# Rotating an 8192 x 8192 matrix: three output buffers, part of the grid in PSUM, and the first output of a macro tile gathered row tile by row tile

## The chip, the cores and the metric

The kernel runs on one core of one Trainium2 chip. The metric is device time in microseconds (us). TensorE is called PE here, VectorE DVE, ScalarE ACT, and SyncE SP. A DMA of this kernel always moves 2 MB (128 partitions of 16 KB). DMAs started by SP run on queue q1, those started by ACT on q10; both queues are served by the same 16 DMA engines.

## The reference

The matrix is rotated by 90 degrees, counterclockwise; no arithmetic is done on its elements.

```python
x = np.random.randn(8192, 8192).astype(np.float32)
k = 1
out = np.rot90(x, k)          # out[i, j] = x[j, 8191 - i]
```

Every element is read once and written once: 268 MB each way.

## The kernel before

The matrix is cut into 16 macro tiles of R = 1024 rows by W = 4096 columns. A macro tile is loaded as T = 8 row tiles of 128 rows (load m = 8 kk + t for row tile t of macro tile kk), and stored as J = 8 outputs (output n = 8 kk + j), each of 512 columns of the macro tile, which are 512 rows of the result. There are 128 loads and 128 outputs, 2 MB each.

Every engine has its own list of instructions, written out by hand, and waits on semaphores:

- **SP** issues the loads in order (L119). A load goes into one of the `bufs`: the first eight turn through four buffers, later ones through buffers 0 and 1. It waits until the load that used the buffer before has been copied out (`s_copy`).
- **DVE** has two kinds of work. `place(m)` (L125 to L131) waits for load m and copies it, 4096 elements per partition in one instruction (L128), into `grid`, a square of 8 by 8 chunks of 512 elements. Macro tiles are written along rows and along columns of the square in turn, so that load n + 8 takes exactly the chunks that output n has just left. Staging (L143) copies from a column of the grid 128 columns of all eight row tiles, in reversed order, into one of two `stage` tiles of 1024 elements: four such copies per output. DVE's order is: place the first eight loads; then for each output four stage copies, then `place(n + 8)`.
- **PE** turns the 128 x 128 blocks of a stage tile by eight transposes (L163, each a matmul with the identity) into PSUM. `ps` holds four quarter outputs, all of PSUM. PE needs a free half of `ps` (`s_free`) for every two stage tiles, and each filled stage (`s_full`).
- **ACT** waits until its output buffer is free (`s_store`, or at the end `s_copy`), copies two quarter outputs at a time, 2048 elements, from PSUM to the buffer (L189, two copies per output), and issues the store (L195). Outputs turn through buffers 2 and 3; the last eight also use 0 and 1.

So DVE can run ahead of ACT by the four quarters in PSUM and two in the stages, and stores can be two deep.

Of the kernel before, what the change touches and what calls it, by code (L numbers as in the profile page):

```python
# [6 lines left out]
P = 128  # L7


R = 1024  # L10
T = R // P
W = 4096
G = 4
J = W // (G * P)


CH = G * P
F = G * R

LOOP = 8  # L20
PAIR = 2


def whole_reads(nc):
# [17 lines left out]
def kernel(tc: tile.TileContext, x: bass.AP, k: bass.AP, out: bass.AP):  # L42
    nc = tc.nc
    assert k == 1, f"only k=1 supported, got {k}"
    nc.at_finalize(whole_reads)

    N, M = x.shape
    dt = x.dtype
    macros = [(r0, c0) for r0 in range(0, N, R) for c0 in range(0, M, W)]
    n_out = len(macros) * J  # L50
    n_load = len(macros) * T

    with tc.tile_critical():  # L53
        ident = nc.alloc_sbuf_tensor("ident", [P, P], dt)
        bufs = [nc.alloc_sbuf_tensor(f"buf{i}", [P, F], dt) for i in range(4)]
        grid = nc.alloc_sbuf_tensor("grid", [P, T * J * CH], dt)
        stage = [nc.alloc_sbuf_tensor(f"stage{i}", [P, R], dt) for i in range(2)]
        ps = nc.alloc_psum_tensor("ps", [P, 4 * R], mybir.dt.float32)

        s_id = nc.alloc_semaphore("s_id")  # L60
        s_land = [nc.alloc_semaphore(f"s_land{i}") for i in range(4)]
        s_store = [nc.alloc_semaphore(f"s_store{i}") for i in range(4)]
        s_copy = nc.alloc_semaphore("s_copy")
        s_full = nc.alloc_semaphore("s_full")
        s_pe = nc.alloc_semaphore("s_pe")
        s_act = nc.alloc_semaphore("s_act")
        s_free = nc.alloc_semaphore("s_free")

        def load_buf(m):
            return m % 4 if m < T else m % 2

        def out_buf(n):
            return 2 + n % 2 if n < n_out - J else (2 + n) % 4

        def slots(t, kk):

            g = grid[:].rearrange("p (a b c) -> p a b c", a=T, b=J)
            return g[:, t, :, :] if kk % 2 == 0 else g[:, :, t, :]  # L80

        def column(j, kk):

            g = grid[:].rearrange("p (a b c) -> p a b c", a=T, b=J)
            return g[:, :, j, :] if kk % 2 == 0 else g[:, j, :, :]

        landed = [0] * 4
        land_wait = []
        for m in range(n_load):
            landed[load_buf(m)] += 16  # L90
            land_wait.append(landed[load_buf(m)])

        with nc.Block() as block:

            @block.gpsimd
            def _(e):
                e.memset(ident[:], 0.0).then_inc(s_id, 1)  # L97
                e.wait_ge(s_id, 1)
                e.affine_select(  # L99
                    out=ident[:],  # L100
                    in_=ident[:],
                    compare_op=mybir.AluOpType.not_equal,
                    fill=1.0,
                    base=0,
                    pattern=[[-1, P]],
                    channel_multiplier=1,
                ).then_inc(s_id, 1)

            @block.sync
            def _(e):  # L110
                last = {}
                for m in range(n_load):
                    b = load_buf(m)
                    if b in last:
                        e.wait_ge(s_copy, last[b] + 1)
                    last[b] = m
                    r0, c0 = macros[m // T]
                    r0 += m % T * P
                    e.dma_start(  # L119
                        out=bufs[b][:], in_=x[r0 : r0 + P, c0 : c0 + W]  # L120
                    ).then_inc(s_land[b], 16)

            @block.vector
            def _(e):
                def place(m):  # L125
                    b = load_buf(m)
                    e.wait_ge(s_land[b], land_wait[m])
                    e.tensor_copy(  # L128
                        out=slots(m % T, m // T),
                        in_=bufs[b][:].rearrange("p (j c) -> p j c", c=CH),  # L130
                    ).then_inc(s_copy, 1)  # L131

                for t in range(T):
                    place(t)
                for n in range(n_out):
                    kk, j = divmod(n, J)
                    for w in range(G):
                        g = n * G + w
                        if w == 0:
                            e.wait_ge(s_copy, T * (kk + 1))  # L140
                        if g >= 2:
                            e.wait_ge(s_pe, g - 1)
                        e.tensor_copy(  # L143
                            out=stage[g % 2][:].rearrange("p (t c) -> p t c", c=P),
                            in_=column(j, kk)[:, :, w * P : (w + 1) * P][:, :, ::-1],
                        ).then_inc(s_full, 1)
                    if n + T < n_load:
                        e.drain()
                        place(n + T)

            @block.tensor
            def _(e):
                turns = e.alloc_register("turns")
                e.wait_ge(s_id, 2)
                e.reg_mov(turns, n_out * G // LOOP)
                with e.While(lambda: e.snap(turns) > 0):
                    for b in range(LOOP):
                        if b % PAIR == 0:
                            e.wait_ge(s_free, 1).then_inc(s_free, -1)
                        e.wait_ge(s_full, 1).then_inc(s_full, -1)  # L160
                        at = (b // PAIR % 2 * PAIR + PAIR - 1 - b % PAIR) * R
                        for t in range(T):
                            i = e.transpose(  # L163
                                ps[:, at + t * P : at + (t + 1) * P],
                                stage[b % 2][:, t * P : (t + 1) * P],
                                ident[:],
                            )
                        i.then_inc(s_pe, 1)
                    e.reg_sub(turns, turns, 1)

            @block.scalar
            def _(e):
                stored = [0] * 4
                e.sem_inc(s_free, 2)
                for n in range(n_out):
                    kk, j = divmod(n, J)
                    b = out_buf(n)
                    if stored[b]:
                        e.wait_ge(s_store[b], stored[b])
                    else:  # L180
                        e.wait_ge(
                            s_copy, 1 + max(m for m in range(n_load) if load_buf(m) == b)
                        )
                    for h in range(0, G, PAIR):
                        p = (n * G + h) // PAIR
                        e.wait_ge(s_pe, n * G + h + PAIR)  # L186
                        at = p % 2 * PAIR * R
                        to = (G - PAIR - h) * R
                        e.copy(  # L189
                            bufs[b][:, to : to + PAIR * R], ps[:, at : at + PAIR * R]  # L190
                        ).then_inc(s_act, 1)
                        e.wait_ge(s_act, p + 1).then_inc(s_free, 1)  # L192
                    r0, c0 = macros[kk]
                    top = M - c0 - (j + 1) * G * P
                    e.dma_start(  # L195
                        out=out[top : top + G * P, r0 : r0 + R].rearrange(
                            "(g m) f -> m g f", g=G
                        ),
                        in_=bufs[b][:].rearrange("m (g f) -> m g f", g=G),
                    ).then_inc(s_store[b], 16)  # L200
                    stored[b] += 16
                for b in range(4):
                    e.wait_ge(s_store[b], stored[b])


# [33 lines left out]
```

## Time and profile before

| | before |
|---|---|
| median of 3 runs | 1273.86 us (1273.26 to 1273.86) |
| the profiled execution: its own time | 1274.23 us |
| its span | 1272.4 us |
| mean granted PE clock | 0.762 |
| PE busy | 722.3 us (57%), 4096 matmuls |
| DVE busy | 627.9 us (49%), 640 copies |
| ACT busy | 479.2 us (38%), 256 copies |
| DMA | 537.00 MB, 422 GB/s over the span |
| a load, issue to landing | 14.5 us (median of 128) |
| a store, issue to landing | 15.7 us (median of 128) |

The span reaches from the first to the last instruction that the profiler saw; the time of the execution is somewhat longer. Times in the timeline are microseconds from the start of the span. A timeline line gives start, duration, engine (a q behind its name means the engine's sequencer, here issuing a DMA), source line, operation, output and input with their shapes, how many instructions are merged, and in brackets the idle time before and what ended it. A line of the waits gives who waited, for whom, us in total, number of times, the longest. In the windows each engine's busy time stands with the number of its instructions in brackets; the last three columns are the granted PE clock, the share of the DMA engines that was busy, and GB/s moved.

### The profile page before, as it was taken

The page shows a single profiled execution, that of the slowest core. Times are in us where ns is not written, and L with a number is a line of the kernel's source. Part 1 is how long each engine was busy: PE and PEld are TensorE (multiplying, and loading weights), DVE is VectorE, ACT ScalarE, POOL GpSimd, SP SyncE. Part 2 cuts the span into 40 slices and gives each one's busy share as a digit, 9 for nine tenths or more (in the row PEclk, how much of TensorE's full clock was granted, in tenths as well). Part 3 has the DMA queues.
Part 4 walks back from the last instruction along what each step waited for, and adds up shares of the span by engine and source line. Part 5 has one row for each costly group of instructions (what it writes and reads, how often), then busy time and mean ns, then how long its engine had stood idle before and what let it go on. Part 6 is the DMA issues. An engine that isn't in the chain of part 4 may idle for free.

```text
span 1272.4 us, 11079 instructions
## 1 busy us (share of the span) xinstructions
PE 722.3 (57%) x4096; PEld 686.5 (54%) x4096; DVE 627.9 (49%) x640; ACT 479.2 (38%) x257; POOL 0.7 (0%) x6
## 2 busy tenths in 40 slices
PE   0446566565665665556655655655655556556664
PEld 0445556555654555545655655545655555546664
DVE  3644545544455445544554445544555445544453
ACT  0233443344333433343333433344333433344365
POOL 0000000000000000000000000000000000000000
PEclk9986767768677677786777687786687786786798
DMA  9999999999999999999999999999999999999989
GB/s 396 379 430 429 430 429 429 430 430 428 429 431 429 430 429 430 429 430 430 426 426 425 414 424 423 425 421 416 429 426 417 430 430 429 429 429 422 419 361 387
DMA packets 36878, 537.00 MB, mean 422 GB/s; under 512 B 4096, under 2 KB 4096, under 8 KB 4096
## 3 DMA queue, kind: packets, MB, share of 16 engines
q1 hardware_dynamic: 18432, 268.44, 50.1%
q10 hardware_dynamic: 18432, 268.44, 49.7%
q14 instruction: 14, 0.11, 0.0%
HBM read 268.44 MB, written 268.44 MB: 422 GB/s over the span
## 4 chain that ended last, share of the span: by engine, by line
DMA 74%; ACT 20%; issue 1%; ACTq 1%; PE 0%
DMA out_dram<-buf 74%; ACT buf L189 20%; ACTq L195 0%; PE ps L163 0%; ACTq L192 0%; ACT L189 0%; ACTq L186 0%
## 5 line engine op out<-in xcount | busy, mean ns | idle before, releaser
L163 PE MATMUL ps<-ident,stage 128*128 128x128 f32 x4096 | 722.3, 357 | 537.1 <-PEq L160 536.6
L163 PEld LDWEIGHTS ps<-ident,stage 128*128 128x128 f32 x4096 | 686.5, 192 | 572.7 <-issue 571.9
L189 ACT COPY buf<-ps 128x2048 f32<-128x2048 f32 x256 | 477.9, 1867 | 733.2 <-DMA out_dram<-buf 712.5
L143 DVE COPY stage<-grid 128x1024 f32<-128x1024 f32 x512 | 343.1, 690 | 592.3 <-PE ps L163 591.0
L128 DVE COPY grid<-buf 128x4096 f32<-128x4096 f32 x128 | 293.6, 2294 | 38.0 <-DMA buf<-in_x_dram 26.8
L189 ACT ACT_TABLE_LOAD x1 | 1.3, 1283 | 49.4 <-PE ps L163 49.4
L99 POOL TENSOR_SCALAR_AFFINE_SELECT ident<-ident 128x128 f32<-128x128 f32 x1 | 0.3, 294 | 0.2 <-POOL ident L97 0.2
L97 POOL MEMSET ident<- 128x128 f32 x1 | 0.2, 205 | 0.5 <-SPq L53 0.5
L220 POOL MEMSET const-bfloat16-1.0<- 128x1 bf16 x1 | 0.1, 103 | 0.0
L220 POOL MEMSET const-uint8-127<- 128x1 uint8 x1 | 0.1, 102 | 0.0
L220 POOL MEMSET const-float32-0.0<- 128x1 f32 x1 | 0.1, 99 | 0.2 <-issue 0.2
L220 POOL MEMSET const-float32-1.0<- 128x1 f32 x1 | 0.1, 99 | 0.0
## 6 DMA issues: line engine op xcount, KB each, us to landing
buf<-in_x_dram SPq DMA_DIRECT2D x128, 2048.0 KB, 14.5
out_dram<-buf ACTq DMA_DIRECT2D x128, 2048.0 KB, 15.7
```

Source lines behind the costliest of these rows:

```text
L97: e.memset(ident[:], 0.0).then_inc(s_id, 1)
L99: e.affine_select(out=ident[:], in_=ident[:], compare_op=mybir.AluOpType.not_equal, fill=1.0, base=0, pattern=[[-1, P]], channel_multiplier=1,
L128: e.tensor_copy(out=slots(m % T, m // T), in_=bufs[b][:].rearrange("p (j c) -> p j c", c=CH),).then_inc(s_copy, 1)
L143: e.tensor_copy(out=stage[g % 2][:].rearrange("p (t c) -> p t c", c=P), in_=column(j, kk)[:, :, w * P : (w + 1) * P][:, :, ::-1],).then_in ...
L163: i = e.transpose(ps[:, at + t * P : at + (t + 1) * P], stage[b % 2][:, t * P : (t + 1) * P], ident[:],)
L189: e.copy(bufs[b][:, to : to + PAIR * R], ps[:, at : at + PAIR * R]).then_inc(s_act, 1)
L220: nc = _bacc.Bacc("TRN2", target_bir_lowering=False, num_devices=1)
```

## The change

- **Buffers.** There are five `bufs` in place of four. The first nine loads (0 to 8) turn through buffers 0, 1, 2; later ones through 0 and 1. Outputs turn through 2, 3, 4; the last eight use all five.
- **Grid.** Room for the fifth buffer comes from the grid: its corner of 2 by 2 chunks (row and column 6 and 7 of the square) lies in PSUM (`corner`, half of PSUM). Two of the four chunks of SBUF so freed remain at the end of `grid` and serve as the two stages. `ps` shrinks to the other half of PSUM, two quarter outputs.
- **Half stages.** A stage now holds 512 elements, half of a quarter output. An output takes eight stage copies, each with four transposes. PE still waits for a free part of `ps` once for eight transposes.
- **Corner copies.** A stage copy or a place that reaches into the corner becomes two instructions, one for the SBUF part and one for the PSUM part. This concerns rows 6 and 7 of a macro tile (3072 and 1024 elements), and the odd halves of outputs j = 6 and 7 (256 and 256).
- **First output.** Output j = 0 of a macro tile is staged by row tile: a half stage takes the 512 elements of one row tile. For macro tile 0 every row tile is staged straight from its load buffer as it lands, and placed after that. For later macro tiles row tiles 0 to 6 come from the grid and the last from its load buffer; this stands in DVE's order behind the last output of the macro tile before, ahead of the place of that last row tile. ACT copies such an output with a regrouped write.
- **ACT** copies one quarter output at a time (1024 elements), four copies per output.

```diff
-        bufs = [nc.alloc_sbuf_tensor(f"buf{i}", [P, F], dt) for i in range(4)]
-        grid = nc.alloc_sbuf_tensor("grid", [P, T * J * CH], dt)
-        stage = [nc.alloc_sbuf_tensor(f"stage{i}", [P, R], dt) for i in range(2)]
-        ps = nc.alloc_psum_tensor("ps", [P, 4 * R], mybir.dt.float32)
+        bufs = [nc.alloc_sbuf_tensor(f"buf{i}", [P, F], dt) for i in range(5)]
+        grid = nc.alloc_sbuf_tensor("grid", [P, (T * J - 2) * CH], dt)
+        corner = nc.alloc_psum_tensor("corner", [P, 4 * CH], mybir.dt.float32)
+        ps = nc.alloc_psum_tensor("ps", [P, 2 * R], mybir.dt.float32)
...
         def load_buf(m):
-            return m % 4 if m < T else m % 2
+            return m % 3 if m <= T else (m + 1) % 2
 
         def out_buf(n):
-            return 2 + n % 2 if n < n_out - J else (2 + n) % 4
+            e = n - (n_out - J)
+            if e < 0:
+                return 2 + (n + 1) % 3
+            free = [load_buf(n_load - 2), load_buf(n_load - 1)]
+            free += [out_buf(n_out - J - 3 + i) for i in range(3)]
+            return free[e % 5]
...
+                    e.drain()
                     e.wait_ge(s_land[b], land_wait[m])
+                    for at, n, v in pieces(*((0, t) if kk % 2 else (t, 0)), J, kk % 2):
+                        i = e.tensor_copy(out=v, in_=a[:, at : at + n, :])
+                    i.then_inc(s_copy, 1)
+
+                def to_stage(srcs):
+
+                    nonlocal half
+                    if half >= 2:
+                        e.wait_ge(s_pe, half - 1)
+                    for at, v in srcs:
+                        s = stage(half)[:, at * P : at * P + v.shape[1] * v.shape[2]]
+                        i = e.tensor_copy(
+                            out=s.rearrange("p (n c) -> p n c", n=v.shape[1]),
+                            in_=v[:, :, ::-1],
+                        )
+                    i.then_inc(s_full, 1)
+                    half += 1
+
+                def first(kk):
+
+                    for t in range(T):
+                        m = kk * T + t
+                        b = load_buf(m)
+                        if kk == 0 or t == T - 1:
+                            e.wait_ge(s_land[b], land_wait[m])
+                            v = bufs[b][:, :CH].rearrange("p (n c) -> p n c", n=1)
+                        else:
+                            e.wait_ge(s_copy, m + 1)
+                            v = chunks(*((0, t) if kk % 2 else (t, 0)), 1, False)
+                        to_stage([(0, v)])
+                        if kk == 0 or t == T - 1:
+                            place(m)
+
+                first(0)
                 for n in range(n_out):
                     kk, j = divmod(n, J)
...
+                    if j:
+                        e.wait_ge(s_copy, T * (kk + 1))
+                        for w in range(G):
+                            for t in range(0, T, H):
+                                to_stage(
...
+                    if kk + 1 < len(macros):
+                        if j < J - 1:
+                            place(n + T)
+                        else:
+                            first(kk + 1)
...
-                    for h in range(0, G, PAIR):
-                        p = (n * G + h) // PAIR
-                        e.wait_ge(s_pe, n * G + h + PAIR)
-                        at = p % 2 * PAIR * R
-                        to = (G - PAIR - h) * R
-                        e.copy(
-                            bufs[b][:, to : to + PAIR * R], ps[:, at : at + PAIR * R]
-                        ).then_inc(s_act, 1)
-                        e.wait_ge(s_act, p + 1).then_inc(s_free, 1)
+                    for h in range(G):
+                        g = n * G + h
+                        e.wait_ge(s_pe, 2 * g + 2)
+                        src = ps[:, g % 2 * R : (g % 2 + 1) * R]
+                        if j == 0:
+                            src = src.rearrange("p (t g c) -> p t g c", t=2, g=G)
+                            dst = bufs[b][:].rearrange(
+                                "p (g t c) -> p t g c", g=G, t=T
+                            )[:, 2 * h : 2 * h + 2]
+                        else:
+                            dst = bufs[b][:, (G - 1 - h) * R : (G - h) * R]
+                        e.copy(dst, src).then_inc(s_act, 1)
+                        e.wait_ge(s_act, g + 1).then_inc(s_free, 1)
```

`pieces` and `chunks` give the access patterns of a row or column of the grid, cut where it passes into the corner.

## The prediction

> **What bounds the kernel now.** I read first the page's slices and queues, then the waits, then the start in 2 us windows, then the chain and the end by its single instructions.
>
> ```profile
> span 1272.4 us, 11079 instructions
> GB/s 396 379 430 429 430 429 429 430 430 428 429 431 429 430 429 430 429 430 430 426 426 425 414 424 423 425 421 416 429 426 417 430 430 429 429 429 422 419 361 387
> q1 hardware_dynamic: 18432, 268.44, 50.1%
> q10 hardware_dynamic: 18432, 268.44, 49.7%
> ```
>
> Loads (q1) and stores (q10) together fill the DMA engines. The plateau of 429 to 430 GB/s is their limit; no engine's work shows there. 537 MB at 430 is 1249 us, so at most some 23 us can be won: at the start (396, 379), in the dips of the middle (full engines, slower packets; the change has no hold on them), and at the end (361, 387).
>
> ```profile
> 50.00:52.00 2.00, 1.98 (x13) 1.74 (x11) 1.90 (x2) 1.99 (x2) 0.00 (x0) 1.00 0.62 262
> 52.00:54.00 2.00, 0.86 (x8) 0.89 (x9) 1.60 (x3) 1.88 (x2) 0.00 (x0) 1.00 0.60 123
> 54.00:56.00 2.00, 2.00 (x19) 1.77 (x18) 1.49 (x3) 1.14 (x2) 0.00 (x0) 1.00 0.73 303
> 58.00:60.00 2.00, 1.06 (x10) 1.09 (x11) 1.40 (x3) 1.22 (x1) 0.00 (x0) 1.00 0.90 254
> ```
>
> The last column is GB/s: loads have run out of buffers and no store is there yet. From 46 to 62 us the windows miss 811 x 2 us / 429 = **3.8 us** of transfer.
>
> ```profile
> 593.93 15.70 DMA out_dram<-buf
> 613.60 15.75 DMA out_dram<-buf
> ```
>
> This chain follows every second store: 19.7 us for two stores and two loads, **4.92 us per 2 MB transfer**, 9.85 per load and store.
>
> ```profile
> ACT buf L189 <- DMA out_dram<-buf: 712.5, 120, 10.3
> DVE grid L128 <- DMA buf<-in_x_dram: 26.8, 9, 8.2
> ```
>
> ACT waits for old stores at 120 outputs, DVE for loads only 9 times: loads are ahead, stores behind. How far, at the end:
>
> ```profile
> 1192.07 0.33 SPq L119 DMA_DIRECT2D buf<-in_x_dram  x1
> buf<-in_x_dram SPq DMA_DIRECT2D x1, 2048.0 KB, 14.4
> 1202.75 3.85 ACT L189 COPY buf<-ps 128x2048 f32<-128x2048 f32 x2 [5.97 <-DMA out_dram<-buf]
> 1212.64 3.85 ACT L189 COPY buf<-ps 128x2048 f32<-128x2048 f32 x2 [6.04 <-DMA out_dram<-buf]
> ```
>
> Load 126, the last but one, lands at 1192.1 + 14.4 = 1206.5. Counted back from the last issue, 116 stores have landed at 1202.7 and 117 at 1212.6: at 1206.5 it is 116.4. The **lead of loads over stores is 127 - 116.4 = 10.6**, and 243.4 transfers are done. The last store is issued at 1261.9 and takes 9.0: landed 1270.9, **64.4 us after load 126**.
>
> **The change, part by part.**
>
> *Start.* Store 0 no longer waits for place(7) and four stage copies. Load 7 lands at 42.4 (place(7) starts at 42.46); then one 128x512 stage copy. DVE's two sizes, 2.29 us for 4096 and 0.69 for 1024, give 0.52 ns an element and 0.155 fixed: 0.42. Four cold transposes: 16 take about 3.6 before, so 0.95. One ACT copy of 1024. ACT has one size, 1.87 for 2048; half is 0.93, all fixed 1.87; with DVE's fixed part it is 1.01, which I take. Store 0 is issued near 45 instead of 54.6; the table load of 1.28 comes earlier, hidden behind loading. Loads 8, 9 and 10 are under way, 15 us of cover. Gap closed: **-3.8**.
>
> *Middle.* DVE gives 512 stage copies of 0.69 for twice as many of 0.42, ACT 256 of 1.87 for 512 of 1.01. Per output: DVE 8 x 0.42 + 2.3 = 5.7, ACT 4 x 1.01 + 0.4 + issue 0.8 = 5.2, under the period of 9.85: nothing, while it holds. Corner copies touch PSUM, for which DVE has no row: the near bound is SBUF's 0.69 for 1024, the other ACT's PSUM pace 0.91 ns, 1.09; I take 1.09. ACT's regrouped write for a first output has no row either; equal cost, hidden in mid-run. The place of a macro tile's last row moves behind eight more stage copies; queued behind it are the next tile's place, its load on SP, and output 1's stages. From row 6's landing that place ends after 2.95 + 11.7 + 3.0 (steps below), and the freed load's first packet comes 1.3 later: 19.0, against 18.7 when the load between ends (two periods less 1.0 of receipt). The load ring is dry for 0.3 us; stores cover that. Nothing, or 0.3 x 15 = 4 us if they did not.
>
> *The lead.* It changes only while one ring is dry. Before, store 0 moved nothing until load 10 was through (windows 56 to 60): 11 loads ahead. Now it starts at 46.4, behind nine loads, and shares with load 9 until 56.2 (from 62 to 66 us both rings had 50.6% each). Store 1 follows place(8), which waits for load 8 at 47.3 and ends at 49.7; staging to issue takes 7.8 (below), first packet 1.0: 58.5. Load 10 runs alone for 2.3 us, half a transfer: lead **9.5**. In steady state landing of load n+7, place 2.3, stage to issue 7.8, first packet 1.0, 9.85 at half rate, receipt 0.8 bring store n home 21.7 us after load n+7, 2.2 periods: lead 9.2, the floor. I take 9.35, against 10.6. So at load 126's landing 244.65 transfers are done, not 243.4: 1.25 x 4.92 = **+6.2** on that landing. The third store buffer stands empty there: stores are late from staging.
>
> *The end.* With a small lead DMA is short of work, and the chain DVE, PE, ACT sets the pace.
>
> ```profile
> 1239.42 3.86 ACT L189 COPY buf<-ps 128x2048 f32<-128x2048 f32 x2 [0.76 <-PE ps L163]
> 1241.63 3.93 PE L163 MATMUL ps<-ident,stage 128*128 128x128 f32 x32 [0.69 <-PEq L160]
> 1243.39 0.56 ACTq L195 DMA_DIRECT2D out_dram<-buf  x1
> 1244.04 3.86 ACT L189 COPY buf<-ps 128x2048 f32<-128x2048 f32 x2 [0.76 <-PE ps L163]
> ```
>
> Before: 4.62 per output, two copies and an issue. The first copy ends at 1241.29, PE starts 0.34 later; eight transposes take 7 x 0.118 + 0.27 = 1.10. After, PSUM holds two quarter outputs, and one half's loop is copy 1.01 + 0.34 + PE 1.10 + 0.09 = 2.54. Copies start at 0, 1.13, 2.54, 3.67, the last ends at 4.68, the issue adds 0.11 + 0.56 + 0.10: **5.45 per output**; 5.75 for j = 6 and 7, whose odd halves are two copies. From a place to the issue of the output behind it: stage 0.56 and PE 1.10, then those copies: 6.6. After a long idle time PE is cold and 32 matmuls take 6.54 (at 611 us) instead of 3.93; about half of that lies ahead of the last copy: 7.8.
> From load 126's landing: place with corner 2.95; then to the staging of load 127's row 11.7, which is output 119 cold 8.1, its issue 0.67, first copy of output 120 1.01, handoff and PE 1.44, then 0.46; place 3.0; 6.6 to the issue of output 121; 4 x 5.45 + 2 x 5.75 = 33.3 to that of 127; landing 6.7 (a lone store at 1223.5 took that). Sum 64.3. PE stands idle for 3.0 us before output 121: after 2.05 us (at 1222) 32 matmuls took 3.88, after 3.50 (at 611) 6.54. Cold, output 121 would come 7.8 - 6.6 = 1.2 later; I add half, 0.6: **64.9**, against 64.4. The 11.35 transfers then left need only 56.
>
> Two rules bear on this. The Trainium skill, "VectorE: DVE Perf Modes", "Why PSUM operands drop a tier", lets fp32 copies with a PSUM operand run at one element per cycle. By my estimate from its 0.96 GHz a corner copy of 1024 would be 1.22, and the two at the end cost 0.3 more; no row here shows one. "TensorE: Matmul & The Clock Gate", "Why this matters for your kernels", sets the limit of a harmless PE gap at about 3 us: by it the cold cost would be none or all of 1.2. Rows put it between 2.05 and 3.50.
>
> **Sum.** -3.8 + 6.2 + 0.5 = +2.9. The profiled execution took 1274.23 (span 1272.4 and 1.8 around it), 0.4 above the median of 1273.86. Predicted: 1277.2 there, **1276.8** on the median.
>
> **Rivals.** *The lead survives (faster).* The third store buffer lets ACT run on, stores stay the late side, lead 10.6: the start alone counts, 1273.9 - 3.8 + 0.5 = 1270.6. For it: 712 us of waits on stores. Against: nothing rebuilds a lead that a nine-load start gave away. It decides from a lead of 10.4 up. Chance 0.19.
> *A quicker end (same).* Copies of 0.93 make 5.26 per output (7 x 0.19 = 1.3), corner copies 0.69 (0.8), PE warm (0.6): end 62.2, 1273.9 - 3.8 + 6.2 - 2.2 = 1274.1. For it: ACT's fixed part is unknown. Against: DVE has one. Chance 0.26.
> *The start gap stays, the lead as before (slower).* If three load buffers stall loading, 1273.9 + 0.5 = 1274.4, or with the smaller lead 1280.6; loading needs one buffer per 4.9 us and place frees it in 3, so it is part of the slow side, 0.03.
> *Forecast.* 0.52, itself from 1274.8 (lead 9.5, half the quick end) to 1280.0 (lead 9.2: +0.7, cold: +0.6, copies of 1.1, 5.72 per output: 7 x 0.27 = +1.9).
>
> About 0.2%, 2.5 us, is what measurement can tell from no change: 1271.3 and 1276.4. Range: down to 1269.8 for the first rival, up to 1280.7 for the last. Faster 0.19, same 0.26, slower 0.52 + 0.03 = 0.55.
>
> **What would show it.** Right: first store issue near 45 and no window under 380 from 46 to 62; ACT's waits on stores almost gone, DVE's on loads grown to some 200 us (9.85 - 7.8 per output); last issues 5.4 apart; load 126 landing near 1209. Wrong: ACT still waiting hundreds of us for stores (lead kept), issues at the end under 5 us apart, or the dips of the middle moved.

## Result and the profile after

| | before | after |
|---|---|---|
| median | 1273.71 us (4 runs, 1273.26 to 1273.86) | 1283.70 us (4 runs, 1281.25 to 1284.54) |
| ratio | 1 | 1.0076, 95% interval 1.0058 to 1.0093 |
| the profiled execution: own time, span | 1274.23, 1272.4 us | 1281.25, 1279.5 us |

The change costs 10.0 us on the medians, 7.0 us between the two profiled executions. Predicted were 1276.8 us and "slower" at 0.55: the sign holds, the time lies outside the range of 1269.8 to 1280.7. The profiled execution of after is the shortest of its four, so what the trace explains is the 7.0 us; the other 3.0 us of the medians are in no trace.

The page of after: its span, the GB/s of 40 equal slices, the two queues.

```profile
span 1279.5 us, 13148 instructions
GB/s 397 422 427 432 428 431 428 428 431 428 431 406 426 432 426 429 410 426 431 428 430 415 414 428 430 425 412 420 426 428 426 424 425 417 420 430 422 428 323 352
q10 hardware_dynamic: 18432, 268.44, 49.8%
q1 hardware_dynamic: 18432, 268.44, 49.6%
```

The second slice is better than before (422 for 379: the start gap), but the plateau (the level of 428 to 432) now has dips from the 12th slice on (406, 410), where before it was flat to the 19th, and the last two slices are worse (323 and 352 for 361 and 387).

The start in windows of 2 us; the last three columns are the granted PE clock, the DMA share and GB/s.

```profile
46.00:48.00 2.00, 0.00 (x0) 0.00 (x0) 0.59 (x1) 0.00 (x0) 0.00 (x0) 1.00 1.08 459
48.00:50.00 2.00, 0.00 (x0) 0.00 (x0) 2.00 (x3) 0.00 (x0) 0.00 (x0) 1.00 1.02 303
52.00:54.00 2.00, 1.97 (x13) 1.60 (x12) 1.27 (x3) 1.43 (x2) 0.00 (x0) 1.00 0.98 418
58.00:60.00 2.00, 1.50 (x12) 1.30 (x13) 1.37 (x4) 0.51 (x1) 0.00 (x0) 0.99 0.98 418
```

From 46 to 62 us the windows now miss 0.5 us of transfer in place of 3.8. One of them is still under 380: at 48 the engines are full (1.02) and move only 303, so these are slow packets, not idle engines. That pattern comes back below.

The waits (who waits, for whom, us, times, longest):

```profile
ACT buf L260 <- PE ps L228: 747.4, 491, 12.6
DVE grid L161 <- DMA buf<-in_x_dram: 182.1, 97, 5.3
DVE grid L171 <- DMA buf<-in_x_dram: 22.2, 8, 8.3
```

ACT's waits on stores, 712.5 us before, are gone; DVE waits 204 us for loads, 26.8 before. The late side has changed from stores to staging.

The end. In the timeline of SP the issue of load 126:

```profile
1194.72 0.33 SPq L146 DMA_DIRECT2D buf<-in_x_dram  x1
```

its time from issue to landing, the last number, in the DMA view of that window:

```profile
buf<-in_x_dram SPq DMA_DIRECT2D x1, 2048.0 KB, 17.2
```

ACT's timeline, with the issues of outputs 120 to 123 and the first copy of output 121:

```profile
1228.94 0.56 ACTq L264 DMA_DIRECT2D out_dram<-buf  x1
1232.55 1.01 ACT L260 COPY buf<-ps 128x1024 f32<-128x1024 f32 x1 [3.71 <-PE ps L228]
...
1237.79 0.56 ACTq L264 DMA_DIRECT2D out_dram<-buf  x1
...
1243.27 0.56 ACTq L264 DMA_DIRECT2D out_dram<-buf  x1
...
1248.73 0.56 ACTq L264 DMA_DIRECT2D out_dram<-buf  x1
```

and PE's ahead of output 121:

```profile
1230.61 6.03 PE L228 MATMUL ps<-ident,grid 128*128 128x128 f32 x32 [2.82 <-PEq L225]
```

Load 126 lands at 1194.7 + 17.2 = 1211.9 (before 1206.4, predicted "near 1209"). The issues at the end are 5.46 to 5.48 us apart, the last two 5.74 and 5.75. The last store lands at 1277.8, 65.9 us after load 126; before it was 64.5.

**One account for all kernels.** From the packets of each trace I counted: how many 2 MB transfers had been moved at 70 us, and how many 1 us before load 126 landed (one is worth 4.92 us of full engines); by how much the 16 KB packets between these points ran over their usual time, 0.611 us for a load and 0.615 for a store (the medians), summed and divided by 16 engines ("slow packets"); the time in which engines had no packet at all, relative to before ("empty"); and the time from load 126's landing to the last store's.

| kernel | median us | moved at 70 us | moved at load 126 | slow packets | empty | load 126 lands | from there |
|---|---|---|---|---|---|---|---|
| before | 1273.7 | 12.95 | 243.92 | 7.7 | 0 | 1206.4 | 64.5 |
| after | 1283.7 | 13.63 | 244.77 | 12.1 | 0.2 | 1211.9 | 65.9 |
| e5, after again | 1281.4 | 13.63 | 244.87 | 12.7 | 0.0 | 1212.9 | 65.1 |
| e1, plain order | 1281.2 | 13.67 | 245.09 | 9.5 | 0.5 | 1211.0 | 67.1 |
| e2, two output buffers | 1329.5 | 13.62 | 244.25 | 22.1 | 41.0 | 1260.2 | 67.0 |
| e3, no early start | 1284.7 | 13.27 | 245.15 | 14.3 | 0.8 | 1218.4 | 64.2 |
| e4, start alone | 1270.5 | 13.56 | 244.55 | 8.2 | 0.1 | 1207.1 | 62.6 |
| e6, e1 with e2 | 1303.7 | 13.64 | 244.09 | 31.2 | 5.1 | 1232.6 | 70.0 |
| e7, e6, corner in SBUF | 1337.0 | 13.64 | 244.09 | 47.9 | 16.0 | 1260.1 | 70.2 |
| e8, e7, all of PSUM for ps | 1275.9 | 13.64 | 244.63 | 7.6 | -0.2 | 1206.4 | 64.0 |
| e9, stores 2 us early | 1318.5 | 13.04 | 243.12 | 38.4 | 9.0 | 1241.8 | 72.7 |
| e10, stores 1 us early | 1452.1 | 12.95 | 242.46 | 113.5 | 70.8 | 1375.9 | 80.2 |

For after against before: 0.68 transfers more at 70 us, -3.35 us; 0.85 more at load 126, +4.2; slow packets +4.4; empty +0.2. Sum +5.45, measured +5.5 on load 126's landing. The end adds 1.4. The same sum gives the landing of every other row to within 0.2 us. It is bookkeeping: packets and gaps fill the time by construction, so the table says where the time lies, not why, and not that a term can be taken out without another growing.

### The profile page after: what moved, and what is told of

It is laid out like the page before. It is cut to its first block, busy times and chain, and to the rows that moved or that the text cites. A ratio compares the mean times of both kernels' runs of the same rounds, so it can differ in the third digit from the quotient of the medians.

```text
span 1279.5 us, 13148 instructions
## 1 busy us (share of the span) xinstructions
PE 736.8 (58%) x4096; PEld 596.2 (47%) x4096; DVE 754.7 (59%) x1312; ACT 520.2 (41%) x513; POOL 0.7 (0%) x6
## 5 line engine op out<-in xcount | busy, mean ns | idle before, releaser
L228 PE MATMUL ps<-ident,grid 128*128 128x128 f32 x4096 | 736.8, 346 | 533.2 <-PEq L225 520.6
L228 PEld LDWEIGHTS ps<-ident,grid 128*128 128x128 f32 x4096 | 596.2, 179 | 673.6 <-issue 630.8
L260 ACT COPY buf<-ps 128x1024 f32<-128x1024 f32 x512 | 518.9, 1014 | 749.9 <-PE ps L228 747.4
L171 DVE COPY grid<-grid 128x512 f32<-128x512 f32 (+1 forms) x1001 | 399.5, 408 | 307.2 <-PE ps L228 301.2
L161 DVE COPY grid<-buf 128x4096 f32<-128x4096 f32 (+1 forms) x128 | 276.5, 2160 | 185.0 <-DMA buf<-in_x_dram 182.1
L171 DVE COPY grid<-corner 128x256 f32<-128x256 f32 x128 | 53.3, 416 | 0.0
L161 DVE COPY corner<-buf 128x1024 f32<-128x1024 f32 x32 | 39.0, 1220 | 0.0
L171 DVE COPY grid<-buf 128x512 f32<-128x512 f32 x23 | 9.8, 427 | 22.4 <-DMA buf<-in_x_dram 22.2
```

The lines of the kernel that those rows point to most:

```text
L161: i = e.tensor_copy(out=v, in_=a[:, at : at + n, :])
L171: i = e.tensor_copy(out=s.rearrange("p (n c) -> p n c", n=v.shape[1]), in_=v[:, :, ::-1],)
L228: i = e.transpose(ps[:, at : at + P], stage(q)[:, t * P : (t + 1) * P], ident[:],)
L260: e.copy(dst, src).then_inc(s_act, 1)
```

## The experiments

All but e4, e9 and e10 are edits of after; those three are edits of before.

**e1: the plain order at the border of macro tiles.** The last row tile is placed first and the whole first output is then staged from the grid; the early start of macro tile 0 stays.

```diff
-                        if kk == 0 or t == T - 1:
+                        if kk == 0:
...
-                        if j < J - 1:
-                            place(n + T)
-                        else:
+                        place(n + T)
+                        if j == J - 1:
                             first(kk + 1)
```

> The changed kernel with the last row tile of every later macro tile placed before the next first output is staged (the order of before); the start stays gathered. Theory A (the order at the macro borders starves the load ring for some 5 us each time, and the DMA engines then run with slower packets): load 126 lands 3 to 5 us earlier than the 1211.9 of the changed kernel, slow packets at the borders vanish, total about 1279.5. Theory B (only the lead of loads and the pace of the end count): landing of load 126 and total stay within 1.5 us, about 1283.5. The end from load 126 on is 65 in both.

Measured: 1281.24 us (4 runs), ratio 1.0057 (1.0040 to 1.0074). That is 2.5 us under after's median, but the two intervals overlap and the profiled executions are the same within 0.3 us (1281.54 and 1281.25). Neither expectation held whole: load 126 lands 0.9 us earlier, not 3 to 5, and slow packets fall from 12.1 to 9.5, they do not vanish; the end grows from 65.9 to 67.1. In the account the border order costs 2.6 us in slow packets; without it 0.3 transfers more are moved before load 126 lands (1.6 us) and the end is 1.2 longer, so in the traces nothing is left of the gain. How the border at 356 us looks in after, in DVE's timeline:

```profile
355.86 0.43 DVE L171 COPY grid<-buf 128x512 f32<-128x512 f32 x1
356.37 1.76 DVE L161 COPY grid<-buf 128x3072 f32<-128x3072 f32 x1
358.05 1.22 DVE L161 COPY corner<-buf 128x1024 f32<-128x1024 f32 x1
360.25 2.29 DVE L161 COPY grid<-buf 128x4096 f32<-128x4096 f32 x1 [0.98 <-DMA buf<-in_x_dram]
372.91 2.29 DVE L161 COPY grid<-buf 128x4096 f32<-128x4096 f32 x1 [4.53 <-DMA buf<-in_x_dram]
```

The place of load 39 ends at 359.27; load 41 is issued at 359.30, and load 40 lands at 360.22: load 41 was queued 0.9 us ahead. In e1 it was issued at 351.80, 6.9 us ahead of load 40's landing at 358.73. The load queue in after and then in before, in the DMA view from 358.4 to 362.8 us (packets, MB, share of the engines):

```profile
q1 hardware_dynamic: 2, 0.00, 0.0%
q1 hardware_dynamic: 79, 1.29, 68.6%
```

The two packets of after hold a few bytes; no 16 KB packet of a load moves there from 358.2 to 363.0. At each of the 14 borders between 70 us and load 126's landing the load ring (queue q1) is dry like this, for 1.8 to 4.8 us, 3.0 on average; in before it never is for more than 0.65 us, in e1 for 0.6. Two windows of after, 14 us behind the border, and the same two of before:

```profile
372.00:374.00 2.00, 0.00 (x0) 0.00 (x0) 1.09 (x1) 0.00 (x0) 0.00 (x0) 1.00 0.98 319
374.00:376.00 2.00, 0.32 (x2) 0.35 (x3) 1.87 (x3) 0.00 (x0) 0.00 (x0) 0.50 0.95 303
372.00:374.00 2.00, 0.00 (x0) 0.00 (x0) 1.32 (x3) 0.70 (x1) 0.00 (x0) 1.00 1.00 426
374.00:376.00 2.00, 0.49 (x3) 0.52 (x4) 0.00 (x0) 1.88 (x2) 0.00 (x0) 0.84 1.04 442
```

In after the engines are busy, 0.98 and 0.95, and move 319 and 303 GB/s; in before 426 and 442. This is why no view of idle engines shows the loss. Five sixths of after's slow packets fall while the four loads behind a border are under way, half of them in before.

**e2: two output buffers in place of three**, all else as in after.

```diff
-        bufs = [nc.alloc_sbuf_tensor(f"buf{i}", [P, F], dt) for i in range(5)]
+        bufs = [nc.alloc_sbuf_tensor(f"buf{i}", [P, F], dt) for i in range(4)]
...
-                return 2 + (n + 1) % 3
+                return 3 - n % 2
```

> The changed kernel with four buffers instead of five: two for stores in mid-run. The prediction's step says that the third store buffer stands empty because stores are late from staging: same time within 1.5 us, 1282 to 1285.5, ACT's waits on stores still under 30 us. Rival (the third buffer carries something): slower by 3 us or more, with ACT waiting for stores for over 100 us.

Measured: 1329.48 us, ratio 1.0438 (1.0418 to 1.0458), 46 us more than after: the prediction's step missed, the rival held. The waits, and two windows of 2 us at the first border:

```profile
ACT buf L260 <- DMA out_dram<-buf: 368.5, 81, 7.2
```

```profile
126.00:128.00 2.00, 2.00 (x12) 1.67 (x11) 1.40 (x3) 1.01 (x1) 0.00 (x0) 0.56 0.39 164
128.00:130.00 2.00, 0.25 (x3) 0.01 (x1) 2.00 (x2) 1.01 (x1) 0.00 (x0) 1.00 0.00 0
```

Both rings are empty: load 16 landed at 122.9 and load 17 was not issued until 130.4, store 8 not until 129.4. With the border order and half of PSUM, an ACT that waits for a store soon holds up PE and DVE, and with them the place and the next load. The third buffer is needed by this kernel; it does not stand empty.

**e3: no early start.** Macro tile 0 is placed whole, then staged from the grid; the borders stay as in after.

```diff
+                    if kk == 0:
+                        for t in range(T):
+                            place(t)
...
-                        if kk == 0 or t == T - 1:
+                        if kk and t == T - 1:
```

> The changed kernel with all of the first eight loads placed before output 0 is staged; all else as in the changed kernel. Lead theory: the gap at the start returns (+3.8 us) but loads come out of it ahead by about one transfer more than the changed kernel's 9.7, which is worth 4 to 5 us at the landing of load 126; total the same or up to 2 us faster, 1281.5 to 1284. Rival (the early first store is a plain gain of 3.8 us): 1287.5.

Measured: 1284.67 us, ratio 1.0082 (1.0065 to 1.0099). The time is 0.7 us above the range of the lead theory and 2.8 below the rival, and the theory's reason missed: store 0 is issued at 53.6 and the start gives back 1.8 of the 3.35 us, but the transfers moved at load 126 do not fall back to 243.9; they are 245.15, and by landings the lead is 9.5, less than after's 9.7 and not one more. Slow packets are 2.2 more than in after. So the lead in this kernel does not depend on the early store 0; what sets it is taken up below.

**e4: the start alone, in the kernel before.** Output 0 is staged partly from the load buffers while macro tile 0 is loaded; four buffers, four quarters in PSUM and the old order stay.

```diff
+                    if t % 4 >= 2:
+                        b = load_buf(t)
+                        e.wait_ge(s_land[b], land_wait[t])
...
+                        i = e.tensor_copy(
+                            out=stage[g % 2][:, t % 2 * CH : (t % 2 + 1) * CH],
+                            in_=bufs[b][:, :CH][:, ::-1],
+                        )
```

> The kernel before, with nothing changed but output 0, which is gathered from row tiles as they land. Lead theory: the gap at the start closes, store 0 is issued near 49, the lead of loads over stores at the landing of load 126 falls from 10.6 to about 9.8, so that load 126 lands at 1206.7 as before and not earlier; the end after it shortens from 64.4 to about 62 since place no longer waits behind ACT; total near 1271. Rival (gap closed is gap won): load 126 lands at 1202.7, end 64.4, total 1270.

Measured: 1270.46 us (10 runs, 1269.07 to 1273.06), ratio 0.9974 (0.9964 to 0.9983): faster than both kernels. Its page:

```profile
GB/s 396 418 430 429 429 429 429 429 429 430 429 429 430 429 429 429 425 428 428 425 427 421 419 419 417 424 424 429 430 424 421 425 424 428 428 427 424 424 342 388
```

The second slice has the gain (418 for 379) and the plateau stays whole. The lead theory held here: load 126 lands at 1207.1 (1206.7 expected), not at the rival's 1202.7. In the account the start brings 3.0 us, and 0.63 transfers more moved at load 126 take 3.1 back on that landing; but the end falls to 62.6 us, since fewer transfers are left and issues there are still 4.62 us apart. Its profiled execution is the slowest of the ten (1273.06), so of the 3.3 us of the medians the trace shows 1.2.

**e5: after once more**, in one run, to see whether the slow packets belong to the kernel.

> The changed kernel once more, unchanged. If its loss in mid-run is a fixed cost of the order at the macro borders, the packets slower than their usual 0.61 us cost again some 13.6 us between 70 us and the landing of load 126, which is at 1211.9 within 1 us. If it is a matter of how loads and stores happen to meet, both move by 2 us or more, while the lead (9.7) and the end (65.9) stay.

Measured: 1281.36 us; slow packets 12.7 (12.1), load 126 at 1212.9 (1211.9). They do. (The 13.6 of the expectation counts only the packets over their usual time; by that count e5 has 14.5.)

**e6, e7, e8: the way back from after to before in steps.** e6 is e1 with e2's buffers. e7 puts the corner into SBUF, in the room of the buffer that was dropped. e8 gives the PSUM that the corner held back to `ps`.

```diff
-        corner = nc.alloc_psum_tensor("corner", [P, 4 * CH], mybir.dt.float32)
-        ps = nc.alloc_psum_tensor("ps", [P, 2 * R], mybir.dt.float32)
+        corner = nc.alloc_sbuf_tensor("corner", [P, 4 * CH], dt)      # e7, e8
+        ps = nc.alloc_psum_tensor("ps", [P, 4 * R], mybir.dt.float32) # e8
...
-                e.sem_inc(s_free, 2)
+                e.sem_inc(s_free, 4)                                  # e8
```

> The kernel e1 (last row tile placed before the next first output) with four buffers instead of five, two for stores in mid-run. Theory C (the third store buffer is needed only for the new order at the borders, where two outputs are staged one behind the other): no dry DMA at the borders, within 2 us of e1's 1281.2. Rival (two store buffers cost as they did in e2): 1320 or more. The end after load 126 stays 66 to 67.

> e6 with the corner of the grid in SBUF, so that no DVE copy touches PSUM; two quarter outputs in PSUM as in the changed kernel. Corner copies of 1024 fall from 1.22 to 0.69 or into one copy of 2.29, odd halves from 0.71 to 0.42: the end is shorter by 1.2 (two places) and 0.5 (outputs 126 and 127). Total 1 to 2.5 us under e6. Rival (the corner is a main cost of the change, through every border and its two slow columns): 5 us or more under e6.

> e7 with four quarter outputs in PSUM instead of two; copies by ACT still of 1024. If the loop through one half of PSUM (copy 1.01, handoff 0.34, PE 1.10, handoff 0.09) sets the pace at the end, as predicted, the last issues come 5.2 apart instead of 5.47, ACT's own four copies and issue, and the total falls by 2 to 4 us. Rival (the half stages of DVE and PE set the pace): 5.47 stays, total within 1 us of e7.

Measured: e6 1303.69 us (ratio 1.0248, 1.0176 to 1.0319); e7 1337.04 (1.0496, 1.0451 to 1.0542); e8 1275.94 (10 runs; 1.0016, 1.0006 to 1.0025). Both expectations for e6 missed: the third buffer is worth 22 us in the plain order, not nothing and not what it is worth with the border order; e6's four runs spread from 1297 to 1317. Those for e7 missed the sign. For e8 the pace at the end came out as expected, 5.16 us apart for 5.47, but the size of the whole was missed: with two output buffers, four quarters in PSUM for two take 61 us off. The waits of ACT on stores in e7 and in e8:

```profile
ACT buf L259 <- DMA out_dram<-buf: 521.8, 112, 8.3
```

```profile
ACT buf L259 <- DMA out_dram<-buf: 641.7, 118, 8.1
DVE grid L161 <- DMA buf<-in_x_dram: 188.1, 119, 2.5
```

ACT waits for stores in both, even more in e8. The difference is what this wait holds up: with two quarters DVE stands still behind it and loads are issued late; with four, DVE has run ahead and waits for loads instead (188 us, 1.6 each), as an engine does whose loads are on time. Why moving the corner to SBUF alone (e7) costs 33 us over e6 (27.8 between the profiled executions, 17 of them in slow packets) is not settled. In both, loads and stores come to be issued in the same moments (706.6 us: store 64 and load 74 in e7), so that both rings run short together. That alone does not make packets slow: in e6 the outputs whose store was issued within 0.6 us of a load went with 0.22 us of slow packets each, the others with 0.42. In e7 all of them are, so e7 itself can't tell.

**e9 and e10: late stores in the kernel before.** ACT copies a part of the finished output buffer onto itself ahead of each store from 8 to 119: twice 2048 elements (e9), and 1024 more (e10). Nothing else changes: no corner, no border order, no third buffer.

```diff
+                    if J <= n < n_out - J:
+                        for w in (PAIR * R, PAIR * R, R):   # e9 without the last
+                            late += 1
+                            part = bufs[b][:, :w]
+                            e.copy(part, part).then_inc(s_late, 1)
+                            e.wait_ge(s_late, late)
```

> The kernel before, with two more copies of 2048 elements (a part of the output buffer onto itself) on ACT ahead of each store from output 8 to output 119; nothing else is changed. By ACT's row of 1.87 us for 2048 from PSUM they take some 3.9 us, so a store is issued about 2 us before the store ahead of it lands, in place of 5.8. Theory (a store that is issued late, behind a ring that is nearly empty, makes slow packets): 16 KB packets lose 9 to 20 us over the run in place of 7.7, load 126 lands 1 to 12 us later. Rival (the slow packets come with the order at the macro border or with the corner in PSUM, not with the margin): 7 to 9 us of slow packets, time within 2 us of before.

> As the run with two more copies, and a third of 1024 elements (about 1.0 us): a store is issued about 0.9 us before the store ahead of it lands, as at the macro borders of the changed kernel, but at each of 112 stores. Theory: the changed kernel lost 4.4 us more in slow packets at 15 borders, 0.3 us each; at 112 stores that makes 15 to 40 us of slow packets in place of 7.7, and load 126 lands 8 to 33 us later. Rival (border order or PSUM, not the margin): 7 to 9 us of slow packets, time within 2 us of before.

Measured: e9 1318.48 us (ratio 1.0352, 1.0311 to 1.0392), e10 1452.08 (1.1400, 1.1381 to 1.1419). In e9 a store was issued 2.1 us on average before the one ahead of it landed (5.9 in before), and the loads behind it came later too, 3.0 us ahead for 4.8; slow packets are 38.4 us in place of 7.7, the rival's 7 to 9 is out, and even the theory's range was too small. In e10 ACT's time per output, 3.85 + 4.92 + 0.7 us of hand-off and issue, comes near the period of 9.85, transfers stretch, and both rings run dry as well; its stores came out 2.4 us ahead, not 0.9, its loads 2.0, and its 113.5 us of slow packets are far above the theory's 15 to 40. e10 in windows of 4 us:

```profile
608.00:612.00 4.00, 3.38 (x16) 3.41 (x17) 0.69 (x1) 3.77 (x3) 0.00 (x0) 0.50 1.00 430
612.00:616.00 4.00, 2.92 (x18) 2.68 (x16) 3.61 (x4) 3.25 (x4) 0.00 (x0) 0.75 0.64 270
616.00:620.00 4.00, 1.81 (x9) 1.84 (x10) 0.59 (x1) 3.77 (x3) 0.00 (x0) 0.68 0.90 258
```

The first window is the plateau, in the second the engines are partly empty (0.64), and in the third they are busy (0.90) and still move only 258: slow packets again. So late stores make packets slow without any other part of the change. Two rivals lie in the edit itself. The added copies could disturb the DMA: but packets that ran beside one were 0.010 us over their usual time on average in e10 and the others 0.119, in e9 0.023 and 0.020. Loads and stores issued together could be the cause (nearly all in e10): but in e9 the outputs issued so had 0.37 us of slow packets each, the others 0.35. How far ahead the store is issued does tell: in e9 the 65 stores under 2 us ahead went with 0.53 us each, the 11 that were 5 us or more ahead with none; in e7 it is 1.06 at 2 to 3 us and 0.02 at 5 to 6. The loads came later in both edits too, so the share of each ring is open, and so is what in the chip makes the packets slow.

## Why the prediction was wrong, step by step

- **Start: right.** Store 0 was issued at 45.33 ("near 45"); the gap of 3.8 us shrank to 0.5, and 3.35 us came home.
- **Middle, "nothing, while it holds": the step that failed.** The copies were priced well: 0.425 us for 512 on DVE (0.42), 1.014 for 1024 on ACT (1.01), and no engine is near the period. But the prediction held that on slower packets "the change has no hold", and that stores cover a load ring that is dry for 0.3 us. The place of a macro tile's last row ended when it was said to (the freed load was issued 17.4 to 18.4 us after row 6's landing, 17.65 priced); the load's first packet came 2.8 to 3.9 us after its issue, not 1.3, and the ring was dry for 3.0 us, not 0.3. Stores did keep the engines busy meanwhile (empty +0.2), but not at 430 GB/s. In before a store in mid-run is issued 5.8 us or more before the one ahead of it lands, the load behind a border 4.5 to 5.3; in after the third store of a macro tile 0.8 to 5.4, and that load 0.9 to 2.7. The term put at nothing was 4.4 us of slow packets: 2.6 go with the border order (e1). The other 1.8 are open: in e1 every store of the middle is issued over 6 us ahead and no ring is dry for more than 0.6. That the outer bound, "0.3 x 15 = 4 us", comes near 4.4 is luck: ten times the dry time at some 0.1 us each.
- **"The third store buffer stands empty": wrong.** Without it the kernel needs 46 us more (e2), or 22 with the plain order (e6 against e1). ACT's vanished waits say that the buffer is always free in time, not that it is not used.
- **The lead: right in direction, too large.** +6.2 us were predicted from 1.25 transfers; 0.85 were measured, +4.2. By landings the lead went from 10.6 to 9.7, not to 9.35. Of the two reasons given, a lead given away by the early start did not survive e3 (9.5 without that start), and in the kernel before it is worth 0.6 transfers (e4), not 1.25. The other, a floor of 9.2 set by the chain from landing to store, fits e3 and after, but no run changed the chain alone; so far the right direction is in part luck.
- **The end: right but for 1.0 us.** The pace was 5.47 us per output (5.45). From load 126's landing to the end of load 127's staging row took 15.1 us (14.65), and output 121 was issued 7.8 us after its place (6.6, or 7.8 cold; I had added half the difference). PE went cold after 2.82 us of idle time: 32 transposes took 6.03 us.
- **The two rules.** The page's groups of after have the new copies that touch PSUM (busy time and mean ns of one):

```profile
L161 DVE COPY corner<-buf 128x1024 f32<-128x1024 f32 x32 | 39.0, 1220 | 0.0
L171 DVE COPY grid<-corner 128x256 f32<-128x256 f32 x128 | 53.3, 416 | 0.0
```

1.220 us is what my estimate from the Trainium skill, "VectorE: DVE Perf Modes", "Why PSUM operands drop a tier", came to (1.22), not my 1.09 from ACT's pace; a copy of 256 takes 0.416 from PSUM and 0.292 from SBUF. Of the PE gap, "TensorE: Matmul & The Clock Gate", "Why this matters for your kernels", says about 3 us. The case here is 2.82, and PE was cold already (granted clock 0.52 from 1230.6 to 1234.0). The length of the gap does not decide alone: in after 24 transposes behind a gap of 2.09 us took 4.78 us (clock 0.65, from 394.6 on), and 8 behind one of 2.08 took 1.06 (clock 1.00, at 234.9).
- **The sum.** Predicted for the profiled execution 1277.2, measured 1281.25: slow packets +4.4, empty +0.2, start +0.45, end +1.0, lead -2.0 make the 4.05 between them. The medians lie 2.9 further apart, 2.45 of it the profiled execution's distance from its own median.
- **The rivals.** "The lead survives" fell with ACT's waits on stores; "a quicker end" with the 5.47 and the cold PE; the start gap did not stay. None held a loss in the middle. The sign for it was named, "the dips of the middle moved", and it is what happened; I had no case with a chance behind it.

## What to carry to other kernels

Where two DMA rings share full engines, look at how long before a landing the next transfer of that ring is queued, not at idle time: an engine that has 40% of its time free (DVE here) can still issue too late. Room given to buffers is only as good as the run-ahead between the engines behind them: here half of PSUM bought a third output buffer (e1, 1281.2 us) and lost more than it brought (e8, with two output buffers, the corner in SBUF and all of PSUM for `ps`, 1275.9), while the early first output by itself, on the old buffers, is the gain (1270.5 us). Test a claim that "this buffer stands empty" by taking the buffer away.

## What the runs showed of the hardware

Most 16 KB packets take 0.61 us (the median in before and after); in after, packets of some 1.2 us stand around the late transfers at the borders (at 363 and at 373 to 375 us, for instance), with the engines counted as busy all the while. Stores issued 2.1 us ahead in place of 5.9 raised the time lost in slow packets from 7.7 to 38.4 us over a run (e9); the loads were issued later there too, 3.0 us ahead for 4.8.
